# Expert weights of a two-layer mixture of experts in ten loads and 14 ring units instead of five loads and 7

## The chip, the core and the metric

The kernel runs on one core of one Trainium2 chip. The metric is the device time of one execution in microseconds (us). Three runs of the kernel before gave 3209.64, 3211.02 and 3211.98 us; the median is 3211.02 us.

## What is computed

The reference is a network of two blocks in float32, on 256 tokens of width 1024. The first block has two layers; each is a token mixer (attention and spatial gating) followed by a mixture of experts (MoE). The second block has an attention layer and an RWKV layer, each with an MLP, for the tokens and for 256 context tokens. Only the MoE of the first block is touched. Cut to its core:

```python
def moe_ffn(h, router_w, router_bias, w_gate, w_up, w_down, ws_gate, ws_up, ws_down):
    scores = sigmoid(xt @ router_w)                  # 256 tokens, 64 experts
    eidx = top 8 experts of each token, from its best 4 of 8 groups
    ...
    def run_block(args):
        hb = jax.nn.silu(xb @ w_gate[e]) * (xb @ w_up[e])     # 1024 -> 256
        return (hb @ w_down[e]) * ws[:, None]                 # 256 -> 1024
    ...
    shared = (jax.nn.silu(xt @ ws_gate) * (xt @ ws_up)) @ ws_down
    return (routed + shared)
```

Each expert has 3.15 MB of float32 weights: w_gate and w_up of 1024 x 256, w_down of 256 x 1024. Each layer reads all 64 experts, so the two MoE stages move 403 MB of the 748 MB that the kernel moves.

## The kernel before

`moe` (called from `tile_net`, L1867) sorts the experts of a layer by their number of tokens and gives them blocks of three sizes (`CAPS`, L30): 4 experts with 128 token slots, 28 with 64, 32 with 32. A group is 256 slots: 2, 4 or 8 experts; `ORDER` (L32) sets the order of the 13 groups. A group is computed in two pairs of 128 slots, so a pair holds 1, 2 or 4 experts side by side.

For each pair, `fetch` (L683 to L698) reads the expert numbers into registers of the SP queue and issues the loads there. `up` (L836) multiplies the gathered tokens `xe` by gate and up into `gu`: eight steps j over the width, and within each step all the pair's experts. `down` (L864) multiplies by w_down into `yps`. `scatter` adds the result to the tokens. Each matmul is carried out as two instructions in the trace, so the 64 experts of a layer give 1024 instructions in `gu` and 512 in `yps`.

The weights lie in a ring in SBUF, made by `weights` (L92) with a number of buffers; `wbuf` (L82) hands out the next unit of `WU` = 2048 floats per partition, which is 8 KB, or 1 MB over 128 partitions. The ring of an MoE stage has 7 units. An expert takes three units:

```python
gus = [[self.wtile([2, 4, 256], [((v,), src(n, u, KT)[:, 4 * a:4 * a + 4, :])
                                 for v, n in enumerate(("w_gate", "w_up"))], "gu")
        for u in range(k)] for a in range(2)]
dn = [self.wtile([2, D], [(None, src("w_down", u, 2))], "dn") for u in range(k)]
```

Two units hold gate and up, each for four of the eight steps j, and are filled by two loads of 512 KB with rows of 4 KB; one holds w_down, filled by one load of 1 MB with rows of 8 KB. A unit is refilled when the last matmul that reads it has ended. All these loads stand in one queue, SP's, in program order, so one that waits for its unit holds up those behind it.

Beside the experts, `side_work` (L1890) issues work of the second block's context path (attention, MLP with `mu` and `w`, RWKV features with `rk`, `rsc`, `r`, `zy`). Its matmuls and loads stand in the same queues. A scheduler fixes the order of each engine's instructions when the kernel is built. `overflow` handles experts with more tokens than their slots by gathers (`wild_weights`, L769); its loads `wgu` and `wdn` do not appear in the trace.

Of the kernel before, what the change touches and what calls it, by code (L numbers as in the profile page):

```python
# [21 lines left out]
P = 128  # L22
D = 1024
# [8 lines left out]
ORDER = (128, 64, 32, 64, 64, 32, 64, 32, 64, 64, 32, 64, 128)  # L32
WU = 2048
WP = 1024
BG_MIX = 4
BG_GROUP = {128: 0, 64: 12, 32: 40}

# [5 lines left out]
class Net:  # L43
    def __init__(self, ctx, tc, inp, consts, out):
        self.ctx, self.tc, self.nc, self.i, self.cst, self.out = ctx, tc, tc.nc, inp, consts, out
        self.side = "left"
        self.whi, self.wp = None, WP
        self.atag = ("acc", 4)
        self.ttag = ("tr", 2)
        self.pending = ()  # L50
        pool = lambda name, bufs, **k: ctx.enter_context(self.pool(name=name, bufs=bufs, **k))
        self.const = pool("const", 1)
        self.res = pool("res", 2)
        self.ps = pool("ps", 1, space=PSUM)
        self.sm = pool("sm", 2)
        self.dram = pool("dram", 1, space=bass.MemoryType.DRAM)
        self.setup()
# [24 lines left out]
    def wbuf(self, shape, name):  # L82
        n = 1
        for v in shape:
            n *= v
        t = self.wts.tile([P, WU], F32, tag="w", name=name)
        v = t[:, :n]
        if len(shape) > 1:
            dims = " ".join(f"d{q}" for q in range(len(shape)))
            v = v.rearrange(f"p ({dims}) -> p {dims}", **{f"d{q}": shape[q] for q in range(len(shape))})  # L90
        return v
    def weights(self, name, bufs, hi=0):  # L92

        st = ExitStack()
        self.wts = st.enter_context(self.pool(name=name, bufs=bufs))
        self.whi = st.enter_context(self.pool(name=name + "h", bufs=hi)) if hi else None
        return st
# [411 lines left out]
    def moe(self, l, x, row, mc, mce, rw, rb):  # L509
# [136 lines left out]
        for t in range(2):  # L646
            self.split(x[:, t, :].rearrange("q (p j) -> q j p", j=KT), xLH, slice(None), t)
        self.racc = x
        wgu = [self.wtile([4, 512], [((slice(None), slice(256 * u, 256 * u + 256)),
                                      dap(i[n], (l * D + 512 * a) * 256, [[256, P], [P * 256, 4], [1, 256]]))  # L650
                                     for u, n in enumerate(("ws_gate", "ws_up"))]) for a in range(2)]
        wd = self.wtile([2, D], [(None, dap(i["ws_down"], l * 256 * D, [[D, P], [P * D, 2], [1, D]]))])
        pg = [self.acc([P, 2, S], "shp") for _ in range(2)]
        for a in range(2):
            for u in range(2):
                for nb_ in range(2):
                    for k in range(4 * a, 4 * a + 4):
                        c = u * 256 + nb_ * P
                        self.mm(pg[u][:, nb_, :], wgu[a][:, k - 4 * a, c:c + P], hT[:, k, :], k == 0 and nb_ == 0,
                                k == KT - 1)  # L660
        sT = pp.tile([P, 2, S], F32, name="sT")
        nc.scalar.activation(sT, pg[0], AF.Silu)
# [1 line left out]
        for h in range(2):  # L664
            for t in range(2):
                ps = self.acc([P, 512], "shd")
                for k in range(2):
                    self.mm(ps, sT[:, k, t * P:(t + 1) * P], wd[:, k, h * 512:h * 512 + 512], k == 0, k == 1)
                nc.scalar.copy(self.racc[:, t, h * 512:h * 512 + 512], ps)
        pre.close()  # L670

# [12 lines left out]
        def fetch(q, pr):  # L684

            r0, w = groups[q]
            k = P // w
            with tc.issue_after(behind.pop(0)) if len(behind) > 1 else ExitStack():
                rvs = [nc.values_load(self.ei[0:1, r0 + pr * k + u:r0 + pr * k + u + 1],
                                      engines=[mybir.EngineType.SP], min_val=0, max_val=NE - 1) for u in range(k)]  # L690
            src = lambda n, u, j: i[n][l, bass.DynSlice(rvs[u], 1)].rearrange("e (p j) f -> p (e j) f", j=j)
            gus = [[self.wtile([2, 4, 256], [((v,), src(n, u, KT)[:, 4 * a:4 * a + 4, :])
                                             for v, n in enumerate(("w_gate", "w_up"))], "gu")
                    for u in range(k)] for a in range(2)]
            dn = [self.wtile([2, D], [(None, src("w_down", u, 2))], "dn") for u in range(k)]
            behind.append(self.load.ins)
            return gus, dn, False

# [45 lines left out]
    def wild(self, l, wio, n, pos, wt, idx, pl):  # L744
        nc = self.nc
        sh = [P, n, NE]
        a = pl.tile(sh, F32, name="wlA")
        b = pl.tile(sh, F32, name="wlB")
        w3 = wio.unsqueeze(2).to_broadcast(sh)
        nc.vector.tensor_tensor(a, w3, self.se[:, 0, :].unsqueeze(1).to_broadcast(sh), op=OP.is_ge)  # L750
        nc.vector.tensor_tensor(b, w3, self.se[:, 1, :].unsqueeze(1).to_broadcast(sh), op=OP.is_lt)
        nc.vector.tensor_tensor(a, a, b, op=OP.mult)
        ofs = pl.tile([P, n], F32, name="wlo")
        nc.vector.tensor_scalar(ofs, wio, 1.0, 64.0, op0=OP.add, op1=OP.mult)
        for t in range(2):
            nc.vector.tensor_tensor(b, a, self.q[:, t, :].unsqueeze(1).to_broadcast(sh), op=OP.mult)
            nc.vector.reduce_sum(pos[:, t, :], b, axis=AX.X)
            nc.vector.tensor_tensor(pos[:, t, :], pos[:, t, :], ofs, op=OP.subtract)
            nc.vector.tensor_tensor(b, a, self.wt[:, t, :].unsqueeze(1).to_broadcast(sh), op=OP.mult)
            nc.vector.reduce_sum(wt[:, t, :], b, axis=AX.X)  # L760
        nc.vector.tensor_tensor(b, a, self.eid.unsqueeze(1).to_broadcast(sh), op=OP.mult)
        ei = pl.tile([P, n], F32, name="wle")
        nc.vector.reduce_sum(ei, b, axis=AX.X)
        nc.vector.tensor_scalar(ei, ei, float(P), float(l * NE * P), op0=OP.mult, op1=OP.add)
        nc.vector.tensor_scalar(idx, ei, self.pf, None, op0=OP.add)

    def wild_weights(self, l, idxs):
        nc, i = self.nc, self.i
        def load(n, ix, nm):  # L769
            t = self.wbuf([WU], nm)  # L770
            nc.gpsimd.indirect_dma_start(out=t, out_offset=None, in_=dap(i[n], 0, [[2048, 2 * NE * P], [1, 2048]]),
                                         in_offset=bass.IndirectOffsetOnAxis(ap=ix, axis=0))
            return t

        gus = [[load(n, ix, "wgu").rearrange("p (a b) -> p a b", b=256) for ix in idxs] for n in ("w_gate", "w_up")]
        dn = [load("w_down", ix, "wdn").rearrange("p (a b) -> p a b", b=D) for ix in idxs]
        return gus, dn, True

    def tables(self, pos, wt, n, pl):
        nc = self.nc  # L780
# [55 lines left out]
    def up(self, g, p_, posT, weights, wk, nb=2):  # L836
# [7 lines left out]
        for j in range(KT):  # L844
            for v in range(2 if wild else 1):
                for u in range(k):
                    if wild:
                        self.mm(gu[w * u:w * u + w, 256 * v:256 * v + 256], sx(j, u), gus[v][u][:, j, :],
                                j == 0 and v == 0, j == KT - 1)
                    else:  # L850
                        self.mm(gu[w * u:w * u + w, :].rearrange("p (a b) -> p a b", a=2), sx(j, u),
                                gus[j // 4][u][:, :, j % 4, :], j == 0, j == KT - 1)
        bp = self.tr([P, S], "bp")
        self.mm(bp, g["eb"][:, P * p_:P * p_ + P], posT, True, True)
        hs = wk.tile([P, 256], F32, tag="hs", name="hs")
# [8 lines left out]
    def down(self, g, p_, hm, ohT, dn, wk, nb=2):  # L864
# [10 lines left out]
        for hf in range(2):  # L875
            sl = slice(hf * 512, hf * 512 + 512)
            y = self.acc([P, 512], "yps")
            for j in range(2):
                for u in range(P // w):
                    self.mm(y[w * u:w * u + w, :], hT[:, j, w * u:w * u + w], dn[u][:, j, sl], j == 0, j == 1)  # L880
            nc.scalar.activation(yH[:, sl], y, AF.Copy, scale=g["wsl"][:, p_:p_ + 1])  # L881
            nc.vector.scalar_tensor_tensor(yL[:, sl], y, g["wsl"][:, p_:p_ + 1], yH[:, sl], op0=OP.mult,  # L882
                                           op1=OP.subtract)
# [20 lines left out]
    def overflow(self, l, mce):  # L904
        nc, tc = self.nc, self.tc
        with self.pool(name=f"ovf{l}", bufs=1) as op:
            cnt = op.tile([P, 2], F32, name="ocnt")
            nc.vector.tensor_copy(cnt, self.iow[:, 0:2])
            with tc.For_i(0, MAXOVER // 2, 1):
                pos = op.tile([P, 2, 2], F32, name="opos")  # L910
                wt = op.tile([P, 2, 2], F32, name="owt")
                idx = op.tile([P, 2], I32, name="oidx")
                self.wild(l, cnt, 2, pos, wt, idx, op)
                pr = self.wild_weights(l, [idx[:, 0:1], idx[:, 1:2]])
                posT, wHL = self.tables(pos, wt, 2, op)
                g = drain_last(self.pick(pos, 0, wHL, mce, op))
                self.down(g, 0, *self.up(g, 0, posT, pr, op, 1), pr[1], op, 1)
# [913 lines left out]
def tile_net(ctx, tc, inp, consts, out):  # L1831
# [30 lines left out]
    with net.pool(name="b1") as net.b1:  # L1862
        for l in range(2):
            with net.weights(f"wm{l}", 4, 2):
                r = net.mixer1(l, x)
            with net.weights(f"we{l}", 7):
                net.moe(l, *r)  # L1867
    with net.weights("w2", 4, 2):
        drain(weave(net.attention(0, (x,), rows[0], kvd), late_path()))
# [64 lines left out]
```

## Time and profile before

| what | value |
|---|---|
| median of three runs | 3211.02 us |
| the profiled execution | 3201.93 us, span 3200.2 us |
| mean granted TensorE clock | 0.925 of full speed |
| TensorE (PE) busy | 2852.5 us, 89% of the span |
| DMA traffic | 748.25 MB, mean 234 GB/s |
| expert loads | 256 of w_gate and 256 of w_up (512 KB), 128 of w_down (1024 KB) |

The first MoE stage lies at about 345 to 1090 us of the span, the second at 1478 to 2110. Line L76 is the helper that records every matmul, and L102 the one that records every load of the ring, so instructions are told apart by the tile that they write: `gu`, `yps`, `gat` (gathered tokens), `sca` (scattered results).

### The profile page before, as it was taken

To read this page: it belongs to the slowest core of one execution; us is meant where nothing else is said; L and a number is where in the kernel's file an instruction comes from. 1 tells how busy PE (TensorE), PEld (TensorE's weight loads), DVE (VectorE), ACT (ScalarE), POOL (GpSimd) and SP (SyncE) were. 2 spreads that over 40 slices of the span, in tenths; PEclk is the share of its full clock that TensorE was granted. 3 is DMA by queue.
4 is the path that set the end of the run, shared out by engine and by line. 5 is a ranking of instruction groups with operands and counts; after the bars stand their busy time and mean duration, and the time that the engine had idled before them with its cause. 6 is when DMAs were issued, how large, how long until landed. Compare 5 with 4: busy or idle time off the path is not lost.

```text
span 3200.2 us, 52870 instructions
## 1 busy us (share of the span) xinstructions
PE 2852.5 (89%) x20518; PEld 1881.4 (59%) x20518; DVE 1710.0 (53%) x3348; ACT 1222.8 (38%) x2237; POOL 455.9 (14%) x653
## 2 busy tenths in 40 slices
PE   5998989988999999999898889789999897878899
PEld 2676533444556567766444444245678785656698
DVE  2656434433444576464334344168866775565576
ACT  2563433232323245433223232124554445453443
POOL 1202000000000001010010110013022204343032
PEclk9999999999999999999899999889989997567899
DMA  9764799899989687554797899875335530002452
GB/s 345 284 214 152 285 346 347 320 386 383 363 305 350 246 320 249 173 168 177 279 343 278 308 339 370 327 256 184 113 113 181 168 122 25 11 9 67 176 189 80
DMA packets 237407, 748.25 MB, mean 234 GB/s; under 512 B 24288, under 2 KB 39560, under 8 KB 208480
## 3 DMA queue, kind: packets, MB, share of 16 engines
q1 hardware_dynamic: 230896, 728.56, 62.8%
q0 software_dynamic: 5920, 15.19, 1.6%
q8 instruction: 165, 2.70, 0.3%
q10 hardware_dynamic: 336, 1.06, 0.1%
q14 instruction: 90, 0.74, 0.1%
HBM read 738.56 MB, written 6.18 MB: 233 GB/s over the span
## 4 chain that ended last, share of the span: by engine, by line
PE 66%; DVE 8%; DMA 6%; ACT 5%; issue 3%; SPq 0%; POOL 0%; DVEq 0%; another core or an unknown queue 0%; ACTq 0%; POOLq 0%
PE gu L76 13%; PE mu L76 9%; PE yps L76 7%; PE w L76 7%; DMA gu<-in_w_up_dram 4%; PE gat L76 3%; PE sca L76 3%; PE rk L76 2%; PE adaps L76 1%; PE ao L76 1%; PE zy L76 1%; PE rv L76 1%; DVE wl L240 1%; PE pg L76 1%; PE rsc L76 1%
## 5 line engine op out<-in xcount | busy, mean ns | idle before, releaser
L240 DVE TENSOR_TENSOR wl<-w,wh 128x1024 fp32r<-128x1024 f32 (+1 forms) x432 | 470.9, 1097 | 308.3 <-ACT wh L239 305.4
L239 ACT CAST wh<-w 128x1024 fp32r<-128x1024 f32 (+1 forms) x432 | 377.8, 882 | 513.8 <-PE mu L76 144.7
L76 PE MATMUL gu<-gu,xe 128*32 128x512 f32 (+2 forms) x2048 | 497.6, 625 | 47.2 <-DMA gu<-in_w_up_dram 47.2
L76 PEld LDWEIGHTS gu<-gu,xe 128*32 128x32 f32 (+2 forms) x2048 | 134.9, 130 | 277.4 <-issue 242.6
L76 PE MATMUL yps<-dn,hTe 128*32 128x512 f32 (+2 forms) x1024 | 258.0, 651 | 3.8 <-ACT hTe L872 3.0
L76 PE MATMUL mu<-hTH,wh 128*128 128x256 f32 x768 | 218.0, 289 | 0.6 <-DVE y L1189 0.4
L76 PE MATMUL mu<-hTL,wh 128*128 128x256 f32 x768 | 216.1, 286 | 0.0
L76 PE MATMUL mu<-hTH,wl 128*128 128x256 f32 x768 | 207.4, 286 | 0.2
L882 DVE SCALAR_TENSOR_TENSOR yL<-yps,wsl,yH 128x512 fp32r<-128x512 f32 x104 | 77.8, 750 | 196.3 <-ACT yH L881 196.1
L76 PEld LDWEIGHTS mu<-hTH,wh 128*128 128x128 f32 x768 | 148.0, 193 | 11.7 <-issue 6.2
L76 PE MATMUL w<-wl,aTH 128*128 128x512 f32 x384 | 152.5, 398 | 1.7 <-DVE wl L240 1.5
L76 PE MATMUL adaps<-adaw,lhs 128*32 128x512 f32 x768 | 125.1, 669 | 31.6 <-DMA adaw<-in_w_ada_dram 20.1
L76 PEld LDWEIGHTS yps<-dn,hTe 128*32 128x32 f32 (+2 forms) x1024 | 74.1, 133 | 132.8 <-issue 122.1
L76 PE MATMUL w<-wh,aTL 128*128 128x512 f32 x384 | 151.0, 394 | 0.0
L76 PEld LDWEIGHTS mu<-hTL,wh 128*128 128x128 f32 x768 | 148.1, 193 | 4.6 <-issue 3.2
L76 PEld LDWEIGHTS mu<-hTH,wl 128*128 128x128 f32 x768 | 142.7, 193 | 7.3 <-issue 3.5
L881 ACT ACTIVATE yH<-yps,wsl 128x512 fp32r<-128x512 f32 x104 | 71.3, 687 | 188.2 <-PE yps L76 161.1
L76 PE MATMUL w<-wh,aTH 128*128 128x512 f32 x384 | 137.1, 398 | 3.2 <-ACT wh L239 2.9
L1074 POOL TENSOR_TENSOR x<-x,opt 128x512 f32<-128x512 f32 x56 | 97.8, 1767 | 251.3 <-DVE opt L1073 251.2
L818 DVE TENSOR_SCALAR xe<-gat,mce 128x256 f32<-128x256 f32 x104 | 56.3, 541 | 119.0 <-ACT xe L816 118.4
L76 PE MATMUL gat<-oh,xL 128*128 128x256 f32 x416 | 113.6, 307 | 1.7 <-ACT PC L1446 1.7
L816 ACT ACTIVATE xe<-gat,mce 128x256 f32<-128x256 f32 x104 | 58.7, 564 | 147.1 <-PE gat L76 86.5
(609 smaller groups left out, 6027.0 us busy)
## 6 DMA issues: line engine op xcount, KB each, us to landing
gu<-in_w_gate_dram SPq DMA_DIRECT2D x256, 512.0 KB, 7.2
gu<-in_w_up_dram SPq DMA_DIRECT2D x256, 512.0 KB, 8.4
dn<-in_w_down_dram SPq DMA_DIRECT2D x128, 1024.0 KB, 10.2
w<-in_mlp_w_dram SPq DMA_DIRECT2D x96, 1024.0 KB, 5.4
adaw<-in_w_ada_dram SPq DMA_DIRECT2D x48, 1024.0 KB, 11.8
adaw<-in_ada_w_dram SPq DMA_DIRECT2D x48, 1024.0 KB, 6.9
w<-in_w_in_dram SPq DMA_DIRECT2D x30, 1024.0 KB, 6.4
w<-in_rwkv_w_rkv_dram SPq DMA_DIRECT2D x20, 1024.0 KB, 5.4
```

Source lines behind the costliest of these rows:

```text
L76: return self.nc.tensor.matmul(out, lhsT, rhs, start=start, stop=stop, skip_group_check=True)
L239: self.nc.scalar.copy(h, f)
L240: self.nc.vector.tensor_tensor(l, f, h, op=OP.subtract)
L816: nc.scalar.activation(xe[:, 0, :], ps[:, 0, :], AF.Identity, scale=mce[:, 1, 2 * jj:2 * jj + 1], bias=mce[:, 0, 2 * jj:2 * jj + 1])
L818: nc.vector.tensor_scalar(xe[:, 1, :], ps[:, 1, :], mce[:, 1, 2 * jj + 1:2 * jj + 2], mce[:, 0, 2 * jj + 1:2 * jj + 2], op0=OP.mult, op1=O ...
L881: nc.scalar.activation(yH[:, sl], y, AF.Copy, scale=g["wsl"][:, p_:p_ + 1])
L882: nc.vector.scalar_tensor_tensor(yL[:, sl], y, g["wsl"][:, p_:p_ + 1], yH[:, sl], op0=OP.mult, op1=OP.subtract)
L1074: (self.nc.vector if last else self.nc.gpsimd).tensor_tensor(x[:, t, sl], x[:, t, sl], tt, op=OP.add)
```

## The change

Ring units of the MoE stages shrink from 8 to 4 KB per partition (`EU` = 1024 floats), and the ring has 14 instead of 7, so it takes the same memory. Gate and up of an expert come in four units of two steps j each (loads of 256 KB with rows of 2 KB), w_down in two units of one 128-row half each (512 KB, rows of 4 KB): ten loads instead of five. The shared expert's weights, loaded through the same ring, are split alike, and the gathers of the overflow path.

```diff
+EU = 1024
...
-        t = self.wts.tile([P, WU], F32, tag="w", name=name)
+        t = self.wts.tile([P, self.wu], F32, tag="w", name=name)
...
-    def weights(self, name, bufs, hi=0):
+    def weights(self, name, bufs, hi=0, wu=WU):
...
+        self.wu = wu
...
-        wgu = [self.wtile([4, 512], [((slice(None), slice(256 * u, 256 * u + 256)),
-                                      dap(i[n], (l * D + 512 * a) * 256, [[256, P], [P * 256, 4], [1, 256]]))
-                                     for u, n in enumerate(("ws_gate", "ws_up"))]) for a in range(2)]
-        wd = self.wtile([2, D], [(None, dap(i["ws_down"], l * 256 * D, [[D, P], [P * D, 2], [1, D]]))])
+        wgu = [self.wtile([2, 512], [((slice(None), slice(256 * u, 256 * u + 256)),
+                                      dap(i[n], (l * D + 256 * a) * 256, [[256, P], [P * 256, 2], [1, 256]]))
+                                     for u, n in enumerate(("ws_gate", "ws_up"))]) for a in range(4)]
+        wd = [self.wtile([D], [(None, dap(i["ws_down"], (l * 256 + k * P) * D, [[D, P], [1, D]]))]) for k in range(2)]
...
-            gus = [[self.wtile([2, 4, 256], [((v,), src(n, u, KT)[:, 4 * a:4 * a + 4, :])
+            gus = [[self.wtile([2, 2, 256], [((v,), src(n, u, KT)[:, 2 * a:2 * a + 2, :])
                                              for v, n in enumerate(("w_gate", "w_up"))], "gu")
-                    for u in range(k)] for a in range(2)]
-            dn = [self.wtile([2, D], [(None, src("w_down", u, 2))], "dn") for u in range(k)]
+                    for u in range(k)] for a in range(4)]
+            dn = [[self.wtile([D], [(None, src("w_down", u, 2)[:, j, :])], "dn") for u in range(k)] for j in range(2)]
...
-                                gus[j // 4][u][:, :, j % 4, :], j == 0, j == KT - 1)
+                                gus[j // 2][u][:, :, j % 2, :], j == 0, j == KT - 1)
...
-                    self.mm(y[w * u:w * u + w, :], hT[:, j, w * u:w * u + w], dn[u][:, j, sl], j == 0, j == 1)
+                    self.mm(y[w * u:w * u + w, :], hT[:, j, w * u:w * u + w], dn[j][u][:, sl], j == 0, j == 1)
...
-            with net.weights(f"we{l}", 7):
+            with net.weights(f"we{l}", 14, wu=EU):
```

The scheduler orders the changed program anew. Three places show it. The first is the SP queue near the start of the first MoE stage. DMAHW0 to DMAHW7 are eight counters on which this queue's loads report their landing, taken in turn; PE is the wait for the ring unit, and DMASW stands for loads of the GpSimd queue. Before, a gate and up pair and the w_down load of one expert:

```order
L102 DMA gu<-in_w_up_dram 128x1024 [waits DMAHW4_49]
L102 ISA
L102 DMA gu<-in_w_gate_dram 128x1024 [waits DMAHW5_49,DMASW4_49]
L102 ISA
L102 DMA gu<-in_w_up_dram 128x1024 [waits DMAHW6_49]
L102 ISA
L102 DMA dn<-in_w_down_dram 128x2048 [waits DMAHW7_49,DMASW3_49]
```

With the change:

```order
L104 DMA gu<-in_w_gate_dram 128x512 [waits DMAHW2_49,DMASW4_49]
L104 ISA
L104 DMA gu<-in_w_up_dram 128x512 [waits DMAHW3_49]
L104 ISA
L104 DMA dn<-in_w_down_dram 128x1024 [waits DMAHW4_49,DMASW3_49]
L104 ISA
L104 DMA dn<-in_w_down_dram 128x1024 [waits DMAHW5_49,DMASW2_49]
```

The loads are half as large, and the same eight counters go round among twice as many.

The second is TensorE at the first pair of four 32-slot experts of the first MoE stage; `atp`, `asps`, `aops` and `adaps` are context work. Before:

```order
L76 MATMUL gu<-gu,xe 32x512 x17
L80 MATMUL atp<-ident,ap 128x128 x4
L76 MATMUL asps<-kT,qT 128x256 x2
L80 MATMUL atp<-ident,ap 128x128 x4
L76 MATMUL aops<-apT,v 64x256 x4
L76 MATMUL adaps<-adaw,lhs_117 32x512 x8
L76 MATMUL gu<-gu,xe 32x512
L76 MATMUL asps<-kT,qT 128x256
L76 MATMUL gu<-gu,xe 32x512
L76 MATMUL asps<-kT,qT 128x256
L76 MATMUL gu<-gu,xe 32x512 x13
```

With the change:

```order
L77 MATMUL gu<-gu,xe 32x512 x18
L81 MATMUL atp<-ident,ap 128x128 x4
L77 MATMUL aops<-apT,v 64x256 x4
L77 MATMUL adaps<-adaw,lhs_117 32x512 x4
L77 MATMUL asps<-kT,qT 128x256
L77 MATMUL adaps<-adaw,lhs_117 32x512 x4
L77 MATMUL asps<-kT,qT 128x256
L77 MATMUL gu<-gu,xe 32x512 x6
L81 MATMUL atp<-ident,ap 128x128 x2
L77 MATMUL gu<-gu,xe 32x512
L81 MATMUL atp<-ident,ap 128x128 x2
```

The 32 steps of the pair, cut before into 17, 1, 1 and 13, are cut into 18, 6, 1 and further pieces, with the context work between them.

The third is TensorE at the first 64-slot group of the second MoE stage. Before, the context path has reached the RWKV score matmuls there (`rsc`):

```order
L76 MATMUL rsc<-ZL,BK 64x64 x2
L80 MATMUL hp<-ident,hm 128x128 x2
L76 MATMUL wps<-wHL,oh 128x8 x4
L76 MATMUL rsc<-ZL,BK 64x64 x6
L76 MATMUL yps<-dn,hTe 64x512 x8
```

With the change it is at the RWKV feature projections (`rk`), which stood in the second token mixer before:

```order
L77 MATMUL rk<-xm,w 128x256 x2
L81 MATMUL hp<-ident,hm 128x128 x2
L77 MATMUL wps<-wHL,oh 128x8 x4
L77 MATMUL rk<-xm,w 128x256 x10
L77 MATMUL yps<-dn,hTe 64x512 x8
```

In SP's order the first MoE stage then carries 17.8 MB of the context MLP's loads (27.3 before), and the second 6.3 MB of the loads of w_rkv (none before); the matmuls are the same in number.

## Rows read from the trace of the kernel before

**Rows 1.** The page, part 1: engine busy time, its share of the span, instructions.
```profile
PE 2852.5 (89%) x20518; PEld 1881.4 (59%) x20518; DVE 1710.0 (53%) x3348; ACT 1222.8 (38%) x2237; POOL 455.9 (14%) x653
```

**Rows 2.** Windows of both MoE stages: us, engines busy, TensorE clock, DMA share, GB/s.
```profile
348.00:620.00 272.00, 253.32 (x1240) 124.46 (x1241) 113.69 (x297) 99.37 (x224) 12.07 (x17) 0.97 0.92 344
620.00:775.00 155.00, 126.65 (x708) 61.86 (x710) 51.17 (x91) 37.86 (x71) 4.35 (x4) 0.92 0.98 376
775.00:1075.00 300.00, 297.05 (x1602) 175.47 (x1595) 126.78 (x211) 91.00 (x158) 3.09 (x5) 1.00 0.93 344
1478.00:1860.00 382.00, 335.70 (x2848) 170.43 (x2847) 147.29 (x343) 110.92 (x226) 38.80 (x89) 0.92 0.82 304
1860.00:1975.00 115.00, 103.37 (x832) 49.82 (x830) 51.91 (x119) 34.62 (x65) 8.10 (x18) 0.97 0.95 356
1975.00:2030.00 55.00, 47.25 (x498) 21.96 (x498) 15.66 (x33) 15.16 (x37) 6.76 (x17) 0.91 0.87 336
2030.00:2082.00 52.00, 41.57 (x195) 15.75 (x190) 9.95 (x18) 5.83 (x11) 0.00 (x0) 0.89 0.96 352
```

**Rows 3.** Chain of waits by line, first MoE stage (300 to 1100 us), then second (1470 to 2130).
```profile
by line: PE gu L76 27.3%; PE yps L76 13.4%; PE mu L76 9.7%; PE w L76 8.6%; PE gat L76 6.7%; PE sca L76 5.6%; DMA gu<-in_w_up_dram 5.0%; PE ao L76 2.6%; PE asps L76 2.0%; PE adaps L76 1.8%; PE aops L76 1.7%; issue 1.0%; DMA w<-in_mlp_w_dram 
by line: PE gu L76 28.3%; PE yps L76 17.7%; DMA gu<-in_w_up_dram 13.9%; PE gat L76 7.8%; PE sca L76 6.7%; issue 3.5%; DMA kTq<-kTd 2.0%; PE rsc L76 2.0%; SPq L102 1.4%; PE sa L76 1.1%; PE rtk L80 1.0%; PE su L76 1.0%; PE hp L80 1.0%; PE r1t
```

**Rows 4.** Chain pieces: start us, us, what; first MoE, then second.
```profile
624.50 6.31 DMA gu<-in_w_up_dram
...
1522.94 3.63 PE gu L76 x16
1527.08 5.22 DMA gu<-in_w_up_dram
1532.43 3.62 PE gu L76 x14
...
1562.89 6.15 DMA gu<-in_w_up_dram
...
1599.41 11.62 DMA gu<-in_w_up_dram
...
1616.40 5.12 PE gu L76 x26
...
1748.13 9.70 DMA gu<-in_w_up_dram
...
1769.32 11.40 DMA gu<-in_w_up_dram
...
2010.59 3.56 PE gu L76 x26
...
2014.44 9.22 DMA gu<-in_w_up_dram
...
2068.72 11.40 DMA gu<-in_w_up_dram
```

**Rows 5.** Waits of the SP queue in the second MoE stage: total us, times, longest.
```profile
SPq L102 <- PE gu L76: 217.3, 51, 13.8
```

**Rows 6.** SP timeline: start us, us, what; loads issued with nothing to wait for.
```profile
1595.17 0.33 SPq L102 DMA_DIRECT2D gu<-in_w_gate_dram  x1
1595.71 0.33 SPq L102 DMA_DIRECT2D gu<-in_w_up_dram  x1
```

**Rows 7.** DMA traffic at full load: rows of 2 KB (3004 us), 4 KB (726), 8 KB (799).
```profile
DMA packets 3902, 7.77 MB, mean 388 GB/s; under 512 B 112, under 2 KB 112, under 8 KB 3901
DMA packets 566, 2.06 MB, mean 412 GB/s; under 512 B 63, under 2 KB 63, under 8 KB 566
DMA packets 285, 2.09 MB, mean 418 GB/s; under 512 B 31, under 2 KB 31, under 8 KB 31
```

**Rows 8.** Tile gu, time from issue to landing of its loads.
```profile
DMA to landing us min/median/max: 3.6/7.9/13.0
```

More of the change, by code (lines that the diff above doesn't have):

```diff
@@ L46, in __init__ @@
         self.side = "left"
-        self.whi, self.wp = None, WP
+        self.whi, self.wp, self.wu = None, WP, WU
         self.atag = ("acc", 4)
@@ L648, in moe @@
         self.racc = x
-        wgu = [self.wtile([4, 512], [((slice(None), slice(256 * u, 256 * u + 256)),
-                                      dap(i[n], (l * D + 512 * a) * 256, [[256, P], [P * 256, 4], [1, 256]]))
-                                     for u, n in enumerate(("ws_gate", "ws_up"))]) for a in range(2)]
-        wd = self.wtile([2, D], [(None, dap(i["ws_down"], l * 256 * D, [[D, P], [P * D, 2], [1, D]]))])
+        wgu = [self.wtile([2, 512], [((slice(None), slice(256 * u, 256 * u + 256)),
+                                      dap(i[n], (l * D + 256 * a) * 256, [[256, P], [P * 256, 2], [1, 256]]))
+                                     for u, n in enumerate(("ws_gate", "ws_up"))]) for a in range(4)]
+        wd = [self.wtile([D], [(None, dap(i["ws_down"], (l * 256 + k * P) * D, [[D, P], [1, D]]))]) for k in range(2)]
         pg = [self.acc([P, 2, S], "shp") for _ in range(2)]
-        for a in range(2):
+        for a in range(4):
             for u in range(2):
                 for nb_ in range(2):
-                    for k in range(4 * a, 4 * a + 4):
+                    for k in range(2 * a, 2 * a + 2):
                         c = u * 256 + nb_ * P
-                        self.mm(pg[u][:, nb_, :], wgu[a][:, k - 4 * a, c:c + P], hT[:, k, :], k == 0 and nb_ == 0,
+                        self.mm(pg[u][:, nb_, :], wgu[a][:, k - 2 * a, c:c + P], hT[:, k, :], k == 0 and nb_ == 0,
                                 k == KT - 1)
@@ L667, in moe @@
                 for k in range(2):
-                    self.mm(ps, sT[:, k, t * P:(t + 1) * P], wd[:, k, h * 512:h * 512 + 512], k == 0, k == 1)
+                    self.mm(ps, sT[:, k, t * P:(t + 1) * P], wd[k][:, h * 512:h * 512 + 512], k == 0, k == 1)
                 nc.scalar.copy(self.racc[:, t, h * 512:h * 512 + 512], ps)
@@ L764, in wild @@
         nc.vector.tensor_scalar(ei, ei, float(P), float(l * NE * P), op0=OP.mult, op1=OP.add)
-        nc.vector.tensor_scalar(idx, ei, self.pf, None, op0=OP.add)
+        for h in range(2):
+            nc.vector.tensor_scalar(ei, ei, self.pf if h == 0 else 0.5, None, op0=OP.add)
+            nc.vector.tensor_scalar(idx[:, :, h], ei, 2.0, None, op0=OP.mult)
     def wild_weights(self, l, idxs):
@@ L769, in load @@
         def load(n, ix, nm):
-            t = self.wbuf([WU], nm)
-            nc.gpsimd.indirect_dma_start(out=t, out_offset=None, in_=dap(i[n], 0, [[2048, 2 * NE * P], [1, 2048]]),
+            t = self.wbuf([EU], nm)
+            nc.gpsimd.indirect_dma_start(out=t, out_offset=None, in_=dap(i[n], 0, [[EU, 4 * NE * P], [1, EU]]),
                                          in_offset=bass.IndirectOffsetOnAxis(ap=ix, axis=0))
             return t
-        gus = [[load(n, ix, "wgu").rearrange("p (a b) -> p a b", b=256) for ix in idxs] for n in ("w_gate", "w_up")]
-        dn = [load("w_down", ix, "wdn").rearrange("p (a b) -> p a b", b=D) for ix in idxs]
-        return gus, dn, True
+        gus = [[[load(n, ix[:, h:h + 1], "wgu").rearrange("p (a b) -> p a b", b=256) for h in range(2)] for ix in idxs]
+               for n in ("w_gate", "w_up")]
+        return gus, [[load("w_down", ix[:, h:h + 1], "wdn") for ix in idxs] for h in range(2)], True
     def tables(self, pos, wt, n, pl):
@@ L847, in up @@
                     if wild:
-                        self.mm(gu[w * u:w * u + w, 256 * v:256 * v + 256], sx(j, u), gus[v][u][:, j, :],
+                        self.mm(gu[w * u:w * u + w, 256 * v:256 * v + 256], sx(j, u), gus[v][u][j // 4][:, j % 4, :],
                                 j == 0 and v == 0, j == KT - 1)
@@ L911, in overflow @@
                 wt = op.tile([P, 2, 2], F32, name="owt")
-                idx = op.tile([P, 2], I32, name="oidx")
+                idx = op.tile([P, 2, 2], I32, name="oidx")
                 self.wild(l, cnt, 2, pos, wt, idx, op)
-                pr = self.wild_weights(l, [idx[:, 0:1], idx[:, 1:2]])
+                pr = self.wild_weights(l, [idx[:, u, :] for u in range(2)])
                 posT, wHL = self.tables(pos, wt, 2, op)
```

## Prediction

> **What bounds the kernel now.** I read the page first, then a table of windows over the MoE stages, then the chain of waits, the SP queue, and the DMA traffic. TensorE is busy 89% of the span [rows 1], so time can only come from its waits, or from a slower clock. The table of windows cuts the two MoE stages into seven stretches [rows 2]. Read in it the PE column against the DMA share. From 775 to 1075 us PE is busy 297 of 300 us: matmuls set the end there. In three stretches (620 to 775, 1860 to 1975 and 2030 to 2082 us) the DMA share is 0.95 to 0.98 and PE is busy only 127 of 155, 103 of 115 and 42 of 52 us: transfers set the end. In the longest one, 1478 to 1860 us, neither is full: PE 336 of 382 us, DMA 0.82, clock 0.92. There each waits for the other through the ring.
>
> The chain says the same in another way [rows 3]: it spends 5.0% of 800 us in the first stage and 13.9% of 660 us in the second on the landing of a load of w_up, so 40 + 92 = 132 us. That time is 15 pieces, four in the first stage and eleven in the second; the first, the last and six more are shown [rows 4]. At 1522.94 us they show how the ring works: 16 instructions of `gu` take 3.63 us, only their end frees two units, the loads are issued, the landing takes another 5.22 us, and the next 14 instructions take 3.62 us. The SP queue waits 217.3 us in the second stage for `gu` matmuls to free a unit [rows 5]: the ring is full nearly always.
>
> **What the change costs.** The packets shrink. At full load the trace has rows of 2, 4 and 8 KB: 388, 412 and 418 GB/s [rows 7]. (The size follows from the row: 7.77 MB in the 3902 - 112 packets above 2 KB is 2.05 KB each; likewise 4.1 and 8.2 KB.) An expert is 2.097 MB of gate and up and 1.049 MB of w_down. Before: 2.097/412 + 1.049/418 = 5.09 + 2.51 = 7.60 us. After: 2.097/388 + 1.049/412 = 5.40 + 2.55 = 7.95 us. That is +0.35 us or 4.6%, and over 128 experts +45 us of transfer time. It is paid only where transfers set the end. The three stretches at a share of 0.95 and more are 322 us; in the first some loads are the context's (27.3 MB of MLP weights in that stage), so I count 290 us: 290 x 0.046 = 13 us. Before the waits in the other stretches I add 3 us (six waits, some 10 us of loads ahead of each). Elsewhere it is hidden: in the stretches at 0.82 to 0.93 by the DMA engines' own idle time, which is 0.08 x 272 + 0.07 x 300 + 0.18 x 382 + 0.13 x 55 = 119 us; if that cover were gone, the whole 45 us would show. Cost taken: 16 us, between 0 and 45.
>
> The number of loads has a price too, apart from their rows. Gate and up in loads of 512 KB run at 412 GB/s and w_down in loads of 1 MB at 418 [rows 7], so with several in flight a load of half the size cost 1.5% at most; I take nothing more for it. The 2 KB row is of 1 MB loads, so a load of 256 KB is not in the trace. The Trainium skill, DMA: Bandwidth & Descriptors, Anatomy of one DMA, gives 2.0 us per DMA plus its bytes at 436 GB/s. With nothing overlapped that is, as an estimate, some 27 us per expert after and 17 before, +10 us each and +1280 us in all; the trace does not agree for the sizes it has, as 3.15 MB at 412 to 418 GB/s pass in 7.6 us. What is left of the rule is that the overlap must last, and a rival below (eight in flight) holds that.
>
> SP issues twice as many loads. Two that wait for nothing start 0.54 us apart [rows 6]; ten take about 5.6 us per expert, under the 7.95 us that the transfers take, so they stay hidden, with 2.3 us to spare. The matmuls are the same in number, and the doubled waits of TensorE are for loads that have landed or that it would wait for anyway: nothing, hidden by the matmuls before them. The shared expert's extra loads, ten in all, are issued before TensorE needs them. The overflow path does not run.
>
> The context work moves from the first stage to the mixer and the second stage. 9.5 MB of MLP loads leave the first (23 us of transfer at 412 GB/s), partly from a stretch that transfers bind, and 6.3 MB join the second, whose first stretch has 0.18 x 382 = 69 us of idle DMA time for them. The matmuls only change place. I take 0, between -10 and +10.
>
> **What the change gains.** A unit is freed after half the matmuls. At 1522.94 us the first half of the 3.63 us would free half the units 1.8 us sooner; and the first piece that TensorE needs is half as large: 1.049/412 = 2.5 us of transfer for a unit now, 0.524/388 = 1.35 us then, 1.2 us less. Together 3.0 us for a wait in a stretch where transfers do not bind. Six of the 15 waits lie there: 1527.08, 1562.89, 1599.41, 1748.13, 1769.32 and 2014.44 us [rows 4]; 6 x 3.0 = 18 us. In the stretches that transfers bind, starting sooner gains nothing, as the next wait takes it back. After a long wait TensorE runs slowly: 26 instructions of `gu` take 5.12 us at 1616.40 and 3.56 us at 2010.59 [rows 4]. A shorter wait may keep the clock up; half of six such losses of 1.6 us is 5 us. Gain taken: 23 us. The ends are 0 (TensorE's order is fixed, so a piece that lands early may stand behind other work) and 66 us, half of all 132.
>
> **Sum.** 16 - 23 = -7 us. The profiled execution's 3201.9 us becomes 3194.9; the median of the runs stands 9.1 us above it, so the forecast is 3211 - 7 = **3204 us**. A measurement can tell a change over 0.2%, which is 6.4 us, so this is at the edge of no change; this case's own range is 3190 to 3217.
>
> **Rivals.**
> *The waits halve.* The second stage's clock of 0.92 and its DMA share of 0.82 speak for it: both have room. Half of 132 us is 66, less 16 of cost: -50, 3161 us. Against it: 9 of 15 waits lie where transfers bind.
>
> *The packets' price binds (slower).* It decides from the point at which the DMA share of the 1478 to 1860 stretch, too, rises above about 0.95: then all 45 us are paid, and the gain is only the 1.2 us per wait, 15 x 1.2 = 18: +27 us, 3238, and 3256 without any gain. For it: the share is already 0.92 and 0.93 in the other two long stretches [rows 2], and the moved context loads fill the second stage. Against it: PE is full from 775 to 1075 us. The Trainium skill, Perfetto Trace Analysis, DMA Optimizations, gives the rule on this side: going from 2 KB to 4 or 8 KB improves throughput, and splitting helps where DMA engines are generally idle. Here they are not idle.
>
> *Eight in flight (slower).* Each load waits for the one eight places earlier to report its landing. Eight gate and up loads were 4.2 MB, and are 2.1 MB, which is 5.4 us at 388 GB/s. The shortest landing is 3.6 us [rows 8], of which 1.3 us is the transfer of 0.524 MB, so about 3 us for half the size: room enough. If under load it grew to 6.4 us, each load would be 1 us / 8 late, 1.25 us per expert; for half of the 128 experts +80 us, 3291 us. The median landing of 7.9 us [rows 8] is mostly queue, so this is unlikely, but nothing in the trace excludes it.
>
> *It does nothing.* The ring holds the same bytes, 14 x 4 KB, so how far ahead it looks is unchanged; where transfers set the end, only their price shows. Cost and gain are then both small: 3211 us, within 0.2%. Against it are the six waits whose release comes sooner.
>
> **Chances.** Forecast 0.32 (0.24 of it faster by more than 0.2%, 0.08 within), halved waits 0.18, nothing 0.10, price 0.30, eight in flight 0.10. So faster 0.42, same 0.18, slower 0.40. The range is 3160 to 3256: from the halved waits to the full price without gain. It leaves out the eight in flight (0.10) and the tails of the other cases, about as much again.
>
> **What would show it.** Right: the w_up waits of the chain fall from 132 to about 110 us, the DMA share rises by some 0.03 in the 0.82 stretch, the mean packet rate at full load lies near 388 to 395 GB/s, and the clock of the second stage rises above 0.93. Halved waits: below 70 us. Price: chain waits grow, and lie in stretches at a share of 0.95 or more. Eight in flight: SP waits for landings instead of for `gu` matmuls, with the DMA share falling. I am wrong altogether if PE's busy time changes by more than 20 us, or if the time comes from the second block, where nothing but the order changes.

## The result, and the profile after

The changed kernel takes 3234.6 us (median of 4 runs) against 3210.3 us of the kernel before: ratio 1.0088, 95% interval 1.0068 to 1.0109. It is slower by 24 us by the medians, 28 by the ratio. Ratios are taken over fast runs alone, while the medians below include one slow run each in e5 (3406.9 us) and e6 (6411.7 us). The profiled execution has a span of 3232.3 us (3200.2 before) and a mean granted clock of 0.933 (0.925).

The page's first part answers to [rows 1]:

```profile
PE 2912.0 (90%) x20518; PEld 1881.1 (58%) x20518; DVE 1704.4 (53%) x3348; ACT 1226.5 (38%) x2241; POOL 455.8 (14%) x653
```

TensorE has the same 20518 instructions and is busy 59.5 us longer. The groups of instructions by line say which ones (count, busy us, mean ns of one, idle us before). Before:

```profile
L76 PE MATMUL gu<-gu,xe 128*32 128x512 f32 (+2 forms) x2048 | 497.6, 625 | 47.2 <-DMA gu<-in_w_up_dram 47.2
L76 PE MATMUL yps<-dn,hTe 128*32 128x512 f32 (+2 forms) x1024 | 258.0, 651 | 3.8 <-ACT hTe L872 3.0
```

After:

```profile
L77 PE MATMUL gu<-gu,xe 128*32 128x512 f32 (+2 forms) x2048 | 528.2, 602 | 12.6 <-DMA gu<-in_w_up_dram 12.6
L77 PE MATMUL yps<-dn,hTe 128*32 128x512 f32 (+2 forms) x1024 | 287.0, 629 | 3.7 <-ACT hTe L876 2.5
```

Read three things. The idle time for w_up loads fell from 47.2 to 12.6 us, as finer units should do. One instruction got no longer (602 against 625 ns). Yet the groups are busy 30.6 and 29.0 us more: fewer of them run at the same time. A stretch of TensorE's timeline after the change shows how (start us, us, what, count, idle before):

```profile
1559.59 1.05 PE L77 MATMUL gu<-gu,xe 128*32 128x512 f32 x2
1560.56 1.13 PE L77 MATMUL lora<-xm,lw 128*128 128x256 f32 x4
1561.62 2.05 PE L77 MATMUL gu<-gu,xe 128*32 128x512 f32 x16
1563.99 1.02 PE L77 MATMUL gu<-gu,xe 128*32 128x512 f32 x2 [0.32 <-DMA gu<-in_w_up_dram]
1565.95 1.02 PE L77 MATMUL gu<-gu,xe 128*32 128x512 f32 x2 [0.94 <-DMA gu<-in_w_up_dram]
1567.20 1.07 PE L77 MATMUL gu<-gu,xe 128*32 128x512 f32 x8 [0.23 <-DMA gu<-in_w_up_dram]
```

A step of four 32-slot experts is eight instructions, two for each. They write different 32 rows of `gu` and run side by side: eight take 1.07 us, and two, of one expert alone, take 1.02. At 1559.59 the first expert of a step has been put ahead of context work (`lora`), and its 1.05 us buy a quarter of what they could. At 1563.99 and 1565.95 one expert runs alone, each after a wait for its own load. (The last line ends with the window: two more instructions follow at once.) The Trainium skill, TensorE: Matmul & The Clock Gate, Why this matters for your kernels, says that narrow matmuls whose outputs start at different multiples of 32 partitions run at once (2.38 times as fast for three). The trace agrees (four experts in 1.07 us, one in 1.02), as long as they follow each other.

A step whose matmuls follow each other is one piece; other work between them cuts it into more. Counted over TensorE's order as built, the steps of `gu` and `yps` of two or four experts stood in 139 pieces too many before, and in 245 after. The places are the boundaries of the ring units. In `gu`, 27 cut steps were step 0 and 33 step 4 before; now 19, 21, 28 and 23 are step 0, 2, 4 and 6 (and one is step 1). In `yps`, the second half of w_down had 2 cut steps, and has 31. So twice as many units give twice as many places at which a step can be cut.

The windows of the MoE stages and of the start of the second block (columns as in [rows 2]), before:

```profile
354.00:1110.00 756.00, 706.05 (x3645) 377.79 (x3644) 310.93 (x617) 234.51 (x465) 22.43 (x31) 0.97 0.91 339
1488.00:2130.00 642.00, 565.22 (x4491) 272.75 (x4489) 241.71 (x528) 171.48 (x349) 54.65 (x126) 0.93 0.86 319
2130.00:2350.00 220.00, 191.18 (x1606) 128.42 (x1605) 179.94 (x460) 114.52 (x254) 46.62 (x68) 0.91 0.45 154
```

After:

```profile
357.00:1097.00 740.00, 696.94 (x3370) 341.41 (x3370) 279.65 (x571) 211.93 (x427) 20.71 (x30) 0.98 0.94 334
1440.00:2132.00 692.00, 657.04 (x4291) 313.46 (x4290) 258.70 (x547) 182.62 (x361) 53.13 (x121) 0.97 0.89 313
2132.00:2377.00 245.00, 197.89 (x1780) 134.24 (x1779) 188.33 (x486) 121.86 (x275) 49.25 (x80) 0.86 0.40 138
```

TensorE's idle time in the two stages fell from 50 + 77 to 43 + 35 us, 49 us less. Both kernels begin the last `yps` instruction of the second MoE stage at the same time, 2130 and 2131 us: what the waits gave, the cut steps took. The loss in the span is the rest, from there to the end: 1070 us before, 1101 after. The changed kernel has 496 matmul instructions more to do in it (9100 against 8604), but TensorE is busy only 8 us longer there:

```profile
2129.90:3200.20 1070.30, 931.42 (x8604) 753.48 (x8602) 738.45 (x1363) 504.25 (x930) 290.22 (x357) 0.86 0.34 113
2131.30:3232.30 1101.00, 939.08 (x9100) 759.08 (x9098) 750.57 (x1411) 514.32 (x958) 297.48 (x375) 0.86 0.33 110
```

In its first part, up to the first `mu` matmul of the block's MLP, there are 25 us of the 31, with only 7 us more of busy TensorE.

The chain of waits through the second stage (1440 to 2150 us), by line, answers to [rows 3]:

```profile
by line: PE gu L77 27.6%; PE yps L77 16.9%; PE gat L77 6.8%; PE sca L77 6.3%; DMA gu<-in_w_gate_dram 4.3%; PE rv L77 4.0%; DMA gu<-in_w_up_dram 3.0%; PE rsc L77 2.4%; issue 1.9%; SPq L104 1.9%; PE rk L77 1.6%; DVE ZL L1462 1.5%; PE su L77 1
```

7.3% of 710 us, 52 us, are landings of gate and up (21 us of them w_up); before, w_up alone had 92. The SP queue waits less for `gu` [rows 5], and for something else more (total us, times, longest; second stage):

```profile
SPq L104 <- PE gu L77: 63.0, 37, 9.6
SPq L104 <- DMA dn<-in_w_down_dram: 49.3, 64, 1.9
SPq L104 <- DMA gu<-in_w_gate_dram: 27.8, 83, 1.8
SPq L104 <- DMA gu<-in_w_up_dram: 14.8, 28, 2.9
```

The last three are waits for the landing of an earlier load. I come back to them.

### The profile page after: what moved, and what is told of

It reads as the page before. It is cut to its first block, busy times and chain, and to the rows that moved or that the text cites. A ratio compares the mean times of both kernels' runs of the same rounds, so it can differ in the third digit from the quotient of the medians.

```text
span 3232.3 us, 55427 instructions
## 1 busy us (share of the span) xinstructions
PE 2912.0 (90%) x20518; PEld 1881.1 (58%) x20518; DVE 1704.4 (53%) x3348; ACT 1226.5 (38%) x2241; POOL 455.8 (14%) x653
## 4 chain that ended last, share of the span: by engine, by line
PE 39%; DVE 7%; ACT 4%; DMA 2%; issue 2%; POOL 1%; SPq 0%; another core or an unknown queue 0%; DVEq 0%; ACTq 0%; POOLq 0%
PE gu L77 6%; PE mu L77 6%; PE w L77 4%; PE yps L77 4%; PE rk L77 2%; PE gat L77 2%; PE rv L77 2%; PE sca L77 1%; PE zy L77 1%; PE rsc L77 1%; DVE wl L242 1%; DMA gu<-in_w_gate_dram 1%; PE su L77 1%; PE ro L77 1%; PE sa L77 1%
## 5 line engine op out<-in xcount | busy, mean ns | idle before, releaser
L77 PE MATMUL gu<-gu,xe 128*32 128x512 f32 (+2 forms) x2048 | 528.2, 602 | 12.6 <-DMA gu<-in_w_up_dram 12.6
L77 PE MATMUL yps<-dn,hTe 128*32 128x512 f32 (+2 forms) x1024 | 287.0, 629 | 3.7 <-ACT hTe L876 2.5
L862 DVE TENSOR_TENSOR hm<-hs,gu 128x256 f32<-128x256 f32 x52 | 31.5, 607 | 171.7 <-ACT hs L860 171.7
```

The lines of the kernel that those rows point to most:

```text
L77: return self.nc.tensor.matmul(out, lhsT, rhs, start=start, stop=stop, skip_group_check=True)
L862: nc.vector.tensor_tensor(hm.rearrange("q j p -> q p j"), hs.rearrange("q (p j) -> q p j", j=2), gu[:, 256:].rearrange("q (p j) -> q p j", ...
```

## The experiments

All runs in one table. "Pieces" are those beyond one for each step, counted in TensorE's order; "MoE end" is the start of the last `yps` instruction and "rest" the span less that. The ratio is to the kernel before, measured beside each run, where its median was 3201.6 to 3210.3 us.

| run | pieces | PE busy us | MoE end us | rest us | median us | ratio, 95% interval |
|---|---|---|---|---|---|---|
| before | 139 | 2852.5 | 2130 | 1070 | 3210.3 | 1 |
| after | 245 | 2912.0 | 2131 | 1101 | 3234.6 | 1.0088, 1.0068 to 1.0109 |
| e1 | 139 | 2861.6 | 2187 | 1070 | 3258.9 | 1.0178, 1.0160 to 1.0196 |
| e2 | 245 | 2936.0 | 2231 | 1101 | 3333.1 | 1.0421, 1.0404 to 1.0438 |
| e3 | 0 | 2762.0 | 2100 | 1066 | 3169.2 | 0.9905, 0.9890 to 0.9921 |
| e4 | 65 | 2803.6 | 2098 | 1061 | 3167.8 | 0.9899, 0.9884 to 0.9914 |
| e5 | 139 | 2855.8 | 2145 | 1073 | 3221.2 | 1.0045, 1.0027 to 1.0063 |
| e6 | 139 | 3019.6 | 2732 | 1067 | 3796.4 | 1.1794, 1.1741 to 1.1848 |
| e7 | 103 | 2808.4 | 2075 | 1077 | 3156.3 | 0.9841, 0.9816 to 0.9867 |
| e8 | 2 | 2770.3 | 2092 | 1137 | 3235.7 | 1.0092, 1.0069 to 1.0115 |
| e9 | 139 | 2861.7 | 2185 | 1068 | 3247.7 | 1.0127, 1.0102 to 1.0153 |
| e10 | 80 | 2813.9 | 2100 | 1106 | 3207.7 | 1.0010, 0.9995 to 1.0026 |
| e11 | 152 | 2872.1 | 2129 | 1082 | 3216.6 | 1.0041, 1.0028 to 1.0055 |
| e12 | 71 | 2794.8 | 2079 | 1069 | 3148.8 | 0.9818, 0.9793 to 0.9843 |
| e13 | 139 | 2850.8 | 2121 | 1071 | 3194.8 | 0.9961, 0.9947 to 0.9975 |
| e14 | 139 | 2858.1 | 2141 | 1070 | 3203.9 | 1.0002, 0.9982 to 1.0022 |

### Loads and order exchanged (e1, e2)

The order of an engine can be held: each of its instructions is tied behind the one that is to stand ahead of it, an edge of order without a wait. `seq` is TensorE's list in the other kernel's order.

```diff
...
+    for a, b in zip(seq, seq[1:]):
+        tc.add_manual_dep(b, a.name, mybir.DependencyInfo(mybir.DependencyClass.NoSync, mybir.DependencyReason.DATA),
+                          reason="keep_order")
...
```

e1, the change's loads and units with the old order:

> The change's loads and ring, with TensorE's matmuls held in the order of the kernel before (by a table of numbers). Theory 'order' (the loss comes from TensorE's new order: 106 more pieces of steps that stood side by side, and context work left over for the second block): PE busy falls back from 2912 to about 2850 us, and the time is 3185 to 3215 us, as the loads by themselves cost next to nothing. Theory 'price' (the packets of 2 KB and the doubled number of loads cost the 24 us): 3225 to 3250 us, with PE busy at 2850 and more waits for loads.

e2, the old loads and units with the new order:

> The loads and ring of the kernel before, with TensorE's matmuls held in the order of the changed kernel. Theory 'order': PE busy about 2910 us and 3225 to 3260 us; above the changed kernel, if finer units gain anything, since this order was made for them. Theory 'price': 3205 to 3215 us, as before.

Both are slower than either kernel and lie above the ranges of both theories (3258.9 and 3333.1 us), so neither theory holds as it stood. PE busy goes with the order (2862 and 2936 us), and so does the rest: 1066 to 1073 us in every run of the old order, 1101 in both of the new one. But an order made for one set of loads loses by waits under the other. So the loads alone could not be judged by e1.

### The loads alone (e5, e9, e13, e14, e6)

e5 is the old kernel in its old units and order of TensorE, with ten loads and the rows of the change:

```diff
-            gus = [[self.wtile([2, 4, 256], [((v,), src(n, u, KT)[:, 4 * a:4 * a + 4, :])
-                                             for v, n in enumerate(("w_gate", "w_up"))], "gu")
+            gus = [[self.wtile([2, 4, 256], [((v, slice(2 * c, 2 * c + 2)), src(n, u, KT)[:, 4 * a + 2 * c:4 * a + 2 * c + 2, :])
+                                             for c in range(2) for v, n in enumerate(("w_gate", "w_up"))], "gu")
...
```

w_down's unit is likewise filled by two loads.

> The kernel before with its 7 units of 8 KB and its order of TensorE's matmuls, but ten loads per expert, with the rows of the change (2 KB for gate and up, 4 KB for w_down): the transfers' price without finer units. Run e1 (units and loads of the change, old order) lost 57 us. Theory 'price': all of that is the transfers', 3245 to 3265 us, and finer units give nothing back. Theory 'fit' (an order of matmuls made for other loads loses by its waits, whatever the packets): the old units fit the old order, so 3205 to 3225 us.

It loses 14 us (0.45%): 3221.2 us, inside the range of "fit" (3205 to 3225). e9 then holds TensorE, VectorE, ScalarE and GpSimd in the old order, with the change's units:

> The change's loads and units, with the instructions of TensorE, VectorE, ScalarE and GpSimd all held in the order of the kernel before; only the loads' queue (SP) is ordered anew. Ten loads in the old units cost 14 us (e5), so what this run adds to 14 us is the work of the finer units. Theory 'gain' (the prediction's 3.0 us per wait): 3190 to 3210 us. Theory 'nothing': 3215 to 3228 us. Theory 'loss' (finer units by themselves cost, as e1 may say with its 57 us): over 3235 us.

41 us slower (by the ratio): "loss". But most of TensorE's waits in 640 to 720 us of e9 (total us, times, longest) are not for expert loads:

```profile
PE hps L81 <- DVE y L975: 19.0, 1, 19.0
PE hp L81 <- DVE hm L862: 11.3, 1, 11.3
PE gu L77 <- DMA gu<-in_w_up_dram: 3.5, 1, 3.5
```

`hps` is context work; it needs `y`, which SP stores to memory (`xcd`) and reads back. In e9's SP queue these stand behind more expert loads (85 and 89 MB of them, counted in the trace, against 81 and 85 in e5):

```profile
664.70 0.82 SPq L1096 DMA_DIRECT2D xcd<-xc  x2
677.81 1.02 SPq L966 DMA_DIRECT2D y<-xcd  x2
```

than in e5's:

```profile
642.97 0.98 SPq L1092 DMA_DIRECT2D xcd<-xc  x2
661.14 0.81 SPq L962 DMA_DIRECT2D y<-xcd  x2
```

So e13 holds SP as well: a load of another kind stands behind the same number of expert bytes as before.

> As e9, but the loads' queue (SP) too keeps the order of the kernel before: each load of another kind stands behind the same number of expert bytes as there. e9 lost 41 us where ten loads in the old units lost 14. Theory 'queue' (what e9 lost beyond 14 us is context transfers standing behind expert loads in SP's new order): at most 14 us slower than before, 3190 to 3217 us. Theory 'units' (finer units by themselves cost): 3235 us or more.

It is 0.39% faster than before, some 12 us, and 53 us faster than e9, which differs from it in SP's order alone. The wait for `y` is short again:

```profile
PE hps L81 <- DVE y L975: 2.9, 1, 2.9
```

Theory "queue" holds. The control is e14, with the old units:

> The control for e13: ten loads with the change's rows in the old units of 8 KB, all five engines in the order of the kernel before. The price of the transfers alone: 14 us as in e5, between 5 and 25 us. e13 less this run is what finer units give or take in themselves: the prediction said a gain of 23 us.

No difference (0.02%, -0.18 to 0.22%), below the 5 to 25 us expected. So the loads' price is nothing that shows in the time, within 6 or 7 us, and the finer units gain the difference, about 13 us. In the DMA engines' time the price is there: from 340 to 2240 us they are busy for a larger share, 0.84 against 0.81, while they move no more per second. First before, then e14:

```profile
340.00:2240.00 1900.00, 1726.44 (x10733) 983.94 (x10732) 880.07 (x1811) 622.39 (x1176) 148.09 (x254) 0.95 0.81 298
340.00:2240.00 1900.00, 1724.09 (x10672) 978.06 (x10671) 869.49 (x1776) 614.87 (x1161) 147.52 (x253) 0.95 0.84 297
```

TensorE's waits for w_up between 340 and 2240 us show the gain, in e14:

```profile
PE gu L76 <- DMA gu<-in_w_up_dram: 43.0, 21, 11.1
```

and in e13:

```profile
PE gu L77 <- DMA gu<-in_w_up_dram: 26.7, 15, 12.5
```

e6 was to tell the number of loads from their rows, by halving each load by partitions:

```diff
...
+                    for h in range(2):
+                        q = slice(64 * h, 64 * h + 64)
+                        self.load = nc.sync.dma_start(v[(q,) + sl], src_[q])
...
```

> As the run before, but each load is halved by partitions (64 and 64) and keeps its rows of 4 and 8 KB: the number of loads alone. If the rows make the price, 3198 to 3212 us; if the number of loads makes it (eight in flight, each half as large), the same time as the run before.

It tells neither: 18% slower, by something of its own (last section).

### The cut steps (e3, e4, e7, e10, e11, e12)

Within a step the scheduler keeps the order in which the matmuls are written. Written in reverse, the expert whose load comes last is first, and the others follow at once. e3 does that to the changed kernel, in `gu` and alike in `yps`:

```diff
-                for u in range(k):
+                for u in reversed(range(k)):
...
```

> The changed kernel, but the experts of a pair are taken in reversed order within each step, so that the expert whose load comes last is first and the scheduler cuts no step (245 extra pieces become 0). Theory 'order': 245 pieces at 60 us / 106 = 0.57 us are 140 us, so PE busy falls to about 2770 us and the time to 3120 to 3190 us, what is missing from 140 us being waits for the last load of a step. Theory 'price': the loads set the end, so PE busy falls but its waits grow as much: 3220 to 3240 us.

No step is cut, and PE busy is 2762.0 us, as theory "order" had it. The time is 3169.2, within its range. The timeline shows whole steps and what keeps the rest of the gain:

```profile
1556.30 1.93 PE L77 MATMUL gu<-gu,xe 128*32 128x512 f32 x16
1564.96 2.16 PE L77 MATMUL gu<-gu,xe 128*32 128x512 f32 x16 [1.19 <-DMA gu<-in_w_up_dram]
1571.75 3.60 PE L77 MATMUL gu<-gu,xe 128*32 128x512 f32 x16 [3.57 <-DMA gu<-in_w_up_dram]
```

TensorE now waits for the last load of a step, and after the wait of 3.57 us the same 16 instructions take 3.60 us. Their window has a granted clock of 0.67, a mix of its two levels of 1.2 and 2.4 GHz; it was 1.00, the upper level, at 1556:

```profile
1556.00:1558.50 2.50, 2.50 (x25) 0.70 (x28) 0.00 (x0) 0.77 (x2) 0.00 (x0) 1.00 0.49 192
1571.50:1575.50 4.00, 3.60 (x16) 1.24 (x16) 0.00 (x0) 0.00 (x0) 0.00 (x0) 0.67 1.07 358
```

e4 is the same cure for the kernel before, as far as its seven units can hold whole steps (`range(k) if k > 2 else reversed(range(k))` in `gu`, all of `yps`):

> The kernel before, but the experts of a pair are taken in reversed order in gate and up of two-expert pairs and in all of w_down; gate and up of four-expert pairs stay as they were, since seven units cannot hold whole steps of them. 139 extra pieces become 65. Theory 'order': 74 x 0.57 = 42 us less PE busy, some of it given back as waits: 3170 to 3200 us, and slower than the changed loads with whole steps. Theory 'price': about 3210 us, and faster than the changed loads with whole steps.

PE busy falls by 49 us (42 expected), and the time to 3167.8, 2 us under theory "order"'s range. It is not slower than e3, which that theory wanted, so this pair gives the finer units no gain.

e7 reverses only where the change put new boundaries (`j % 4 == 2` in `gu`, `j == 1` in `yps`):

> The changed kernel, with reversed experts only in the steps at the boundaries that the change adds (steps 2 and 6 of gate and up, the second half of w_down): the scheduler leaves 103 extra pieces instead of 245 (139 in the kernel before). Theory 'order' (the added boundaries make the loss): PE busy 2912 - 142 x 0.57 = 2831 us, and 3180 to 3215 us. Rival: the cuts at the new boundaries cost nothing and the whole gain of e3 came from the old ones: 3220 to 3240 us.

It beats both kernels: 0.9841, some 51 us faster than before and 78 faster than the change. PE busy is 2808.4, lower than the 2831 worked out, and the time is below the expected 3180 to 3215. Curing the new boundaries gives back more than the change's whole loss, so the rival, that the cuts there cost nothing, is refuted. The run does not isolate them: its 103 pieces are fewer than before's 139, and all other work is ordered anew too. e12 heals all of `yps` as well:

> e7 with all of w_down's steps whole too: 71 extra pieces instead of 103. If each piece counts: PE busy 18 us below e7's and 3140 to 3155 us; if whole steps now only wait for the last load, as in e3: 3155 to 3170 us.

14 us less PE busy and 3148.8 us, the fastest of all (0.9818; its interval overlaps with e7's). e10 and e11 heal gate and up, and w_down, alone:

> The changed kernel with reversed experts in gate and up alone: the 149 extra pieces there become 0, of w_down's 80 are left. At 0.57 us a piece PE busy is 2912 - 165 x 0.57 = 2818 us and the time, by what e3 kept of its gain (65 of 150 us), 3155 to 3190 us. If only the places that the change adds matter, about half of e7's gain: 3185 to 3205 us.

> The changed kernel with reversed experts in w_down alone: 6 extra pieces there instead of 96, 146 in gate and up. PE busy 2912 - 93 x 0.57 = 2859 us; 3190 to 3215 us. If w_down's cuts are hidden behind waits for loads: 3225 to 3240 us.

PE busy came out at 2813.9 (2818 expected) and 2872.1 (2859). Over all kernels with an order of their own PE busy rises with the pieces, from 2762.0 us at 0 to 2912.0 at 245: 150 / 245 = 0.61 us each. The times missed: 3216.6 is 1.6 us above e11's range, and 3207.7 is above e10's ranges, though its MoE end is e3's, 2100 us. Its rest is 1106 us. The length of the second block thus changes by tens of us with the scheduler's order, without a change there.

### More context work (e8)

```diff
-            bg = BG_GROUP[groups[q][1]]
+            bg = BG_GROUP[groups[q][1]] * (1.3 if l else 1)
...
```

> e3 (changed loads, whole steps) with 1.3 times as much context work issued beside the second layer's experts, where e3 leaves TensorE idle for 91 us. If that idle time can take the work: 3130 to 3160 us, with the second block shorter by 20 us or more; if the context work delays the experts as much: 3165 to 3180 us.

Neither: the MoE end is 8 us earlier than e3's, and the rest 71 us longer. The work left for the rest does not set its length. e7 and then e8, from the MoE end:

```profile
2075.40:3152.10 1076.70, 932.19 (x9100) 757.11 (x9098) 748.43 (x1411) 514.43 (x958) 296.69 (x375) 0.87 0.34 114
2092.30:3229.50 1137.20, 937.95 (x8596) 762.15 (x8594) 744.17 (x1363) 513.95 (x935) 285.82 (x361) 0.84 0.33 109
```

e7 has the 9100 matmul instructions of the changed kernel and is 24 us shorter there; e8 has as few as the kernel before and is the longest. TensorE's busy time there is nearly equal, so the difference is its idle time; what brings it stays open.

## Why the prediction was wrong

Forecast 3204 us, -7; measured +24, by the medians.

- **The step that failed** is "The matmuls only change place. I take 0, between -10 and +10", and with it "The matmuls are the same in number ...: nothing". The same matmuls in another order took 60 us more of TensorE, and the second block 31 us more. The order rows ahead of the prediction had it: 17, 1, 1 and 13 matmuls became 18, 6, 1 and so on (32 matmuls, four in each of eight steps, where the text there says 32 steps), and the prediction did not ask what a lone one costs.
- **The sum of cost and gain** held in its sign. With all orders held, units and loads together give 12 us (e13), 0.25 to 0.53% or 8 to 17 us, against the 7 forecast. That it came so near is in part luck: cost and gain were both taken too high.
- **The cost**, 16 us, is too high: the rate per full DMA share fell by 5%, from 319 / 0.86 = 371 to 313 / 0.89 = 352 GB/s (4.6% forecast), but e14 shows 0, within 7 us. In e5, where SP and the other engines were ordered anew, 14 us show.
- **The gain**, 23 us, is mis-sized too: about 13 us between e14 and e13. In the changed kernel the waits shrank more: 49 us of idle TensorE in the stages.
- **The price rival** named 3238 us, near the measured time, by another mechanism: e14 excludes it as the cause. That the range of 3160 to 3256 holds 3234.6 is therefore luck: its upper end was that rival's. **Eight in flight** did come, in part. SP's waits for landings of expert loads between 340 and 2240 us were 29 before, 28 us in all:

```profile
SPq L102 <- DMA dn<-in_w_down_dram: 14.5, 10, 2.3
SPq L102 <- DMA gu<-in_w_up_dram: 8.3, 11, 1.5
SPq L102 <- DMA gu<-in_w_gate_dram: 5.4, 8, 0.9
```

  In e14 they are 434:

```profile
SPq L102 <- DMA dn<-in_w_down_dram: 75.1, 104, 2.2
SPq L102 <- DMA gu<-in_w_gate_dram: 71.8, 217, 1.9
SPq L102 <- DMA gu<-in_w_up_dram: 36.7, 113, 1.5
```

  Those 184 us cost nothing there, and the DMA share rose (0.81 to 0.84), where that rival required it to fall.
- **What would show it**: the share of the second stage is up by 0.03 and its clock at 0.97, as the signs of "right" had it, but its chain waits fell from 92 to 52 us (w_up alone to 21), where 22 us less were forecast for both stages together. That points past "right" towards "halved waits"; the chain after the change does not pass through the first stage, so the sum of both can't be had. The full-load rate was to be 388 to 395 GB/s, and a window below has 375. The two signs of "wrong altogether" were PE busy by more than 20 us, and time from the second block. They were the ones that told.
- **Smaller slips**: ten issues at 0.54 us are 5.4 us, not 5.6. The 2.0 us per DMA that the prediction takes from the Trainium skill, DMA: Bandwidth & Descriptors, Anatomy of one DMA, are given there for DMAs issued from GpSimd, while SP issues these loads. The 2 KB against 4 or 8 KB of the Trainium skill, Perfetto Trace Analysis, DMA Optimizations, are sizes of whole DMAs there, not of the rows of loads of 256 KB. No term of the sum rests on either.

How the loss of 24 us divides among TensorE's cut steps, SP's order and the second block stays open to this extent: the new order as a whole costs about 24 + 12 = 36 us against held orders; e7 wins 78 us by curing the new boundaries, which also orders the rest anew. That the scheduler's own model of the loads' landing makes it send the first expert ahead is inferred from the places of the cuts and from e3, not seen.

## What to carry to other kernels

Where a scheduler orders the program, a change of a load's size changes the order of everything; compare how matmuls that share TensorE are grouped before and after, and hold the old order to measure the change itself. When loads become finer, write the matmul that needs the last load first, so that a group that runs side by side starts together. Smaller units can still be right: with whole steps at the new boundaries they were 1.6 to 1.8% faster than before.

## What was not expected of the hardware

Loads over 64 partitions move far less, at the same full DMA share. A window of e6 at full load (2.7 thousand packets, rows of 4 and 8 KB):

```profile
700.00:740.00 40.00, 28.86 (x135) 16.38 (x131) 12.92 (x21) 8.23 (x15) 3.75 (x3) 0.91 1.04 230
```

and one of the changed kernel, whose rows are shorter:

```profile
1570.00:1615.00 45.00, 44.32 (x150) 18.17 (x151) 11.12 (x24) 3.26 (x6) 0.40 (x1) 1.00 1.03 375
```

230 against 375 GB/s; other windows of e6's MoE stages at a share of 0.96 or more have 221 to 245. The Trainium skill, DMA: Bandwidth & Descriptors, Rules for kernel authors, advises one load over 128 partitions in place of two over halves, because the two share the same engines and gain nothing. The run agrees and goes further: they lose 39% of the rate.
